# GpSimd in place of ScalarE and VectorE for the split of the last two input pieces

## The chip, the cores and the metric

The kernel runs on one core of a Trainium2 chip. The core has TensorE (PE, matrix multiplies), VectorE (DVE), ScalarE (ACT), GpSimd (POOL) and SyncE (SP, which here only issues DMAs). Every engine works through its own queue in order, and waits on semaphores for the others. The metric is the device time of one launch in microseconds; lower is better.

## The reference

One layer of a streaming encoder, for a prompt of 1024 tokens and a sample of 64 tokens behind a cache of 128. Only its first stage matters here:

```python
qa, ka, va, qi, ki, wi, qb, kb, vb, ga, gb = mixer_inputs(rmsnorm(xp, norm_mix[l]), pos_p, w_in[l], *norms)
# the indexer, per block of 128 queries
s   = relu(einsum('bqhd,bsd->bqhs', q_i, ki_all))      # 8 heads
isc = einsum('bqh,bqhs->bqs', w, s)                     # score of each key
_, idx = lax.top_k(where(vis, isc, -inf), topk)         # 256 best keys
# attention A over the chosen keys, chunk-band attention B, gates, output, MLP
```

The normalised input is multiplied by the weights `w_in`; some of the columns are the indexer's queries, its key and its head weights. Everything behind (heads' projections, choice of keys, two attentions, output projection, MLP) is left as it is.

## The kernel before

**The input.** x is handed over turned (channels on partitions), and loaded in five pieces: four of 256 tokens, and one of 64, the sample. A piece has two tiles `xc` of four blocks of 128 channels each, so 8 blocks k. The division by the row's root mean square is not applied to x; it is applied to the results later. But `norm_mix` (`g_mix`, one number per channel, so per partition) is multiplied in here. Each block is split in a high part (what TensorE's fp32r format holds) and a low part (the remainder), so that three matrix multiplies (`three`, lines 156 to 158: high x high, high x low, low x high) come near fp32. For piece i and block k, `split_piece` does one ScalarE instruction (line 267: scale, round, write the high part into `xnT`) and one VectorE instruction (line 268: raw times `g_mix` minus the high part, the low part).

**The order.** The framework's scheduler places each engine's instructions at build time, by a timeline of its own and by the order of the code; on the chip the queues then run in that fixed order. `cut_piece(i, raws)` runs `split_piece` over the 8 blocks; for pieces 3 and 4 its instructions stand behind `last["queries"]`, the ScalarE copy that ends the queries' projection before. Around the change the code reads:

```python
stage_queries(4, "s"); stage_queries(5, "s")     # 320 columns, PE 33.3 to 39.3 us
... x4 = take_piece(4); stage_scores(0..2)       # scores of blocks 0 to 2
cut_piece(3, x3)                                 # tokens 768 to 1023
norms(4); norms(5); stage_scores(3)
stage_keys(6); stage_keys(7)                     # need piece 3
norms(6); stage_scores(4); stage_queries(6)
cut_piece(4, x4)                                 # the sample's 64 tokens
xsT copy (line 466), stage_keys(8), norms(7), norms(8), stage_queries(7), stage_queries(8)
```

**What the helpers do.** `stage_keys(i)` projects 128 tokens to the indexer's key, three of its query heads and the head weights; the key lands in a tile `kd`. `stage_norms(i)` (called by `norms`) squares the rows of x (line 281, ScalarE, a tile `xt` of 512 KB in two buffers, so a load of `xt` waits for an older square), works out the scale on VectorE, and finishes the key: rotation on GpSimd (`apply_rope`, lines 211 to 214), copy of the key into the second half of `kd` (line 333). `stage_scores(i)` turns the key on TensorE (line 232, into a PSUM tile `pt`), takes high and low parts (`kih` on ScalarE, `kil` on VectorE, line 234), turns the queries `qd` four heads at a time (line 366, into `pt` as well; `qiT` on ScalarE, its low half on VectorE, line 371), and multiplies (lines 164 and 165, into tiles `s`, one per head). ScalarE applies relu (line 379) and VectorE sums over the heads (lines 381 and 383). There are two `pt` banks, taken in turn; a bank is free when VectorE has read it.

**Names.** In the rows of order below, the keys `kd_290`, `kd_295`, `kd_341`, `kd_378` belong to token blocks 0 to 3, `kd_583` and `kd_620` to 4 and 5. `xc_538`, `xc_539` are piece 3; `xc_774`, `xc_775` are piece 4. `xt_668`, `xt_706` are the rows of blocks 4 and 5; block 6 has `xt_904` before and `xt_912` after, block 7 `xt_942` and `xt_950`, the sample `xt_1114` and `xt_1122`. `pt_784`, `pt_788`, `pt_792` hold the turned keys of blocks 0 to 2, `pt_797` and `pt_804` the turned queries of block 2 (heads 0 to 3, 4 to 7), whose scores begin with `s_811`.

Of the kernel before, what the change touches and what calls it, by code (L numbers as in the profile page):

```python
# [15 lines left out]
ALU = mybir.AluOpType  # L16
# [4 lines left out]
KB = D // P  # L21
# [23 lines left out]
def kernel(  # L45
# [8 lines left out]
    nc = tc.nc  # L54
# [68 lines left out]
    def copy(out, in_):  # L123
        return nc.scalar.activation(out, in_, AF.Copy)  # L124

    last = {}
# [91 lines left out]
    g_mix = ixw.tile([P, KB], F32, name="g_mix")  # L218
# [45 lines left out]
    def split_piece(i, raws, k):  # L264
        c0, n = PIECES[i]
        hi, lo, raw = xnT[:, k, 0, c0:c0 + n], xnT[:, k, 1, c0:c0 + n], raws[k // 4][:, k % 4]
        last["piece"] = nc.scalar.activation(hi, raw, AF.Copy, scale=g_mix[:, k:k + 1])
        nc.vector.scalar_tensor_tensor(lo, raw, g_mix[:, k:k + 1], hi, op0=ALU.mult, op1=ALU.subtract)

# [122 lines left out]
    for j in range(KB // 2):  # L392
        parts["keys"] += split_weights(w_keys, j, j % 2 == 1)
        for k in (2 * j, 2 * j + 1):
            split_piece(0, x0, k)
            for i, ps in enumerate(both):
                tok = slice(i * P, (i + 1) * P)
                three(ps[:, :584 - SPLIT], [((xnT[:, k, 0, tok], xnT[:, k, 1, tok]), parts["keys"][k])], k == 0, k == KB - 1)
# [11 lines left out]
        return raws  # L410

    def cut_piece(i, raws):
        with tc.issue_after(last["queries"].ins) if i > 2 else ExitStack():
            for k in range(KB):
                split_piece(i, raws, k)
# [4 lines left out]
    stage_keys(0)  # L420
    stage_keys(1)
    cut_piece(1, x1)
    for i in (2, 3):
        state[i] = project(i, bank("s"), parts["keys"], 584 - SPLIT)[0]
# [12 lines left out]
    norms(1)  # L437
    x3 = take_piece(3)
    cut_piece(2, x2)
    stage_keys(4)  # L440
    stage_keys(5)
# [4 lines left out]
    with tc.issue_after(last["projected"].ins):  # L446
# [6 lines left out]
        for i in range(3):  # L453
            stage_scores(i)
    cut_piece(3, x3)
    norms(4)
    norms(5)
# [279 lines left out]
    for g in range(0, EARLY, 4):  # L737
        ws = []
        for k in range(KB):
            raw = pj.tile([P, 512], F32, tag="wraw", name="wraw", bufs=2)  # L740
            nc.sync.dma_start(raw, w_in[k * P:(k + 1) * P, C_G + g * P:C_G + g * P + 512])
            hi = pj.tile([P, 512], F32R, tag="whi", name="whi", bufs=11)
            lo = pj.tile([P, 512], F32R, tag="wlo", name="wlo", bufs=11)
# [189 lines left out]
    for mix in "ba":  # L933
        for k in range(4):
            for c0, n in CHUNKS:
                raw = op.tile([P, 384], F32, tag="oraw", name="oraw", bufs=2)[:, :n]
                nc.sync.dma_start(raw, o_dram[mix][k * P:(k + 1) * P, c0:c0 + n])
                hi = oT[mix][:, k, 0, c0:c0 + n]
# [96 lines left out]
    for at_m, m in enumerate(pairs_of_m):  # L1035
# [3 lines left out]
        for ci, (c0, n) in enumerate(CHUNKS):  # L1039
# [17 lines left out]
            k, top, low = m % 4, *(("A11", "A21") if m < 4 else ("A12", "A22"))  # L1057
# [4 lines left out]
            if ci == 1:  # L1062
                hi, lo = (row_blocks[top][:, k, z] for z in range(2))
# [602 lines left out]
```

## Time and profile before

| what | value |
| --- | --- |
| runs | 1682.66 us median of 3 (1681.45 to 1686.31) |
| profiled execution | 1685.72 us, of which 1683.9 us are the span of the core |
| TensorE's mean granted clock | 0.997 of full speed |
| PE busy | 1663.4 us (99%) |
| DVE, ACT, POOL busy | 1200.1, 935.4, 388.2 us |
| ScalarE's share of the splits (line 267) | 32 of 128x256 at 500 ns, 8 of 128x64 at 343 ns |
| VectorE's share of the splits (line 268) | 32 of 128x256 at 555 ns, 8 of 128x64 at 318 ns |

A busy share is an average over stages. The stage with the splits lies in the first 60 us: pieces 0 to 2 are split by 28 us, piece 3 from 39.7 to 44.4 us, piece 4 from 56.3 to 59.8 us. The rows that follow are from that stretch. A timeline row gives the start, the length, the engine, the line, what is written and read, and in brackets how long the engine sat idle before it and what it waited for. Lengths overlap a little with the next instruction's start, so a distance from start to start is the better measure of pace.

### The profile page before, as it was taken

The numbers are of one execution on the slowest core, as the hardware profiler recorded it, in microseconds if no ns is written. First come the engines' busy times: TensorE is split into PE (matmuls) and PEld (weight loads), VectorE is DVE, ScalarE is ACT, GpSimd is POOL, SyncE is SP. The second block draws the span as 40 slices with busy tenths as digits, with TensorE's granted clock in tenths as the row PEclk, the third lists the DMA queues.
The fourth block names the chain that finished last, engine by engine and source line by source line (L and its number), as shares of the span: only waits on it lengthen the run. The fifth ranks groups of instructions, "written<-read, shape, count | busy, mean of one in ns | idle before, by whom it ended". The sixth has DMA issues, their size and how long they took to land.

```text
span 1683.9 us, 29511 instructions
## 1 busy us (share of the span) xinstructions
PE 1663.4 (99%) x10037; PEld 1514.3 (90%) x10037; DVE 1200.1 (71%) x2779; ACT 935.4 (56%) x1870; POOL 388.2 (23%) x534
## 2 busy tenths in 40 slices
PE   9899999999999999999999999999999999999999
PEld 8787888788999999999999879999999988888887
DVE  6854898868868888883456785856687649656794
ACT  6866588796157777774244366544454346343431
POOL 4344223504534434431355420000000000000000
PEclk9999999999999999999999999999999999999999
DMA  7234365673398877645655268555575598765652
GB/s 248 62 123 137 98 189 158 178 248 107 108 214 199 207 179 176 165 111 159 193 163 176 88 213 260 177 179 179 186 229 185 194 315 292 224 203 172 204 181 94
DMA packets 276486, 301.99 MB, mean 179 GB/s; under 512 B 40112, under 2 KB 194224, under 8 KB 276336
## 3 DMA queue, kind: packets, MB, share of 16 engines
q1 hardware_dynamic: 247072, 264.39, 54.1%
q10 hardware_dynamic: 29264, 35.73, 6.0%
q8 instruction: 79, 1.29, 0.3%
q14 instruction: 71, 0.58, 0.1%
HBM read 206.93 MB, written 93.08 MB: 178 GB/s over the span
## 4 chain that ended last, share of the span: by engine, by line
PE 70%; DMA 5%; DVE 3%; ACT 2%; issue 1%; POOL 1%; SPq 0%; ACTq 0%; DVEq 0%; POOLq 0%
PE x L156 6%; PE x L157 6%; PE x L158 6%; PE acc L156 5%; PE acc L158 4%; PE acc L157 4%; PE pt L819 3%; PE pe L156 2%; PE pg L156 2%; PE pg L158 2%; PE pe L158 2%; PE pg L157 2%; PE pe L157 2%; PE po L835 2%; PE s L164 2%; PE s L165 2%
## 5 line engine op out<-in xcount | busy, mean ns | idle before, releaser
L124 ACT ACTIVATE hi<-hw 128x1024 fp32r<-128x1024 f32 (+1 forms) x108 | 100.3, 933 | 161.9 <-PE x L158 52.7
L157 PE MATMUL x<-lo,hi 128*128 128x512 f32 (+1 forms) x440 | 169.5, 385 | 0.0
L158 PE MATMUL x<-hi,lo 128*128 128x512 f32 (+1 forms) x440 | 169.1, 385 | 0.0
L156 PE MATMUL x<-hi 128*128 128x512 f32 (+1 forms) x440 | 164.6, 385 | 0.0
L148 DVE TENSOR_TENSOR lo<-hw,hi 128x1024 fp32r<-128x1024 f32 (+1 forms) x108 | 113.9, 1060 | 50.9 <-ACT hi L124 49.8
L622 ACT ACTIVATE nth<-work,cand 128x768 bf16<-128x768 f32 (+2 forms) x93 | 96.6, 1038 | 14.4 <-DVE cand L640 8.1
L831 DVE TENSOR_TENSOR pl<-pt,ph 128x512 fp32r<-128x512 f32 (+2 forms) x152 | 91.1, 614 | 10.8 <-ACT ph L124 10.4
L156 PEld LDWEIGHTS x<-hi 128*128 128x128 f32 x440 | 82.6, 188 | 16.6
L157 PEld LDWEIGHTS x<-lo,hi 128*128 128x128 f32 x440 | 82.7, 188 | 16.6
L158 PEld LDWEIGHTS x<-hi,lo 128*128 128x128 f32 x440 | 82.6, 188 | 16.5
L124 ACT ACTIVATE ph<-pt 128x512 fp32r<-128x512 f32 (+3 forms) x168 | 80.1, 513 | 31.1 <-PE pt L819 22.6
L156 PE MATMUL acc<-xnT,hi 128*128 128x384 f32 (+1 forms) x288 | 96.2, 334 | 0.2 <-DVE gate L689 0.2
L158 PE MATMUL acc<-xnT,lo 128*128 128x384 f32 (+1 forms) x288 | 94.4, 328 | 0.0
L157 PE MATMUL wide<-wlo,xnT 128*128 128x512 f32 x240 | 94.2, 394 | 0.0
L157 PE MATMUL acc<-xnT,hi 128*128 128x384 f32 (+1 forms) x288 | 94.2, 327 | 0.0
L158 PE MATMUL wide<-whi,xnT 128*128 128x512 f32 x240 | 93.8, 391 | 0.0
L156 PE MATMUL wide<-whi,xnT 128*128 128x512 f32 x240 | 92.2, 394 | 0.8 <-DVE work_s L383 0.8
L806 POOL TENSOR_SCALAR mw<-mw,sm 128x640 f32<-128x640 f32 (+1 forms) x64 | 56.4, 882 | 118.2 <-DVE sm L805 106.0
L835 PE MATMUL po<-pl,vhl 128*128 128x256 f32 (+1 forms) x304 | 78.6, 291 | 0.3 <-DVE pl L831 0.3
L834 PE MATMUL po<-ph,vhl 128*128 128x256 f32 (+1 forms) x304 | 77.9, 274 | 0.0
L150 POOL TENSOR_TENSOR wlo<-wraw,whi 128x512 fp32r<-128x512 f32 x40 | 51.7, 1291 | 111.1 <-ACT whi L124 111.0
L164 PE MATMUL s<-kh,qT 128*128 128x384 f32 (+4 forms) x208 | 76.3, 368 | 0.5 <-DVE sm L799 0.5
(775 smaller groups left out, 5630.8 us busy)
## 6 DMA issues: line engine op xcount, KB each, us to landing
hw<-h SPq DMA_DIRECT2D x108, 256.0 KB, 3.2
hw<-in_w_down_dram SPq DMA_DIRECT2D x108, 256.0 KB, 3.6
wraw<-in_w_in_dram SPq DMA_DIRECT2D x56, 256.0 KB, 2.8
h<-h ACTq DMA_DIRECT2D x32, 272.0 KB, 2.1
raw<-in_w_up_dram SPq DMA_DIRECT2D x32, 256.0 KB, 3.3
out_dram<-t SPq DMA_DIRECT2D x24, 256.0 KB, 2.6
raw<-in_w_in_dram SPq DMA_DIRECT2D x24, 256.0 KB, 3.8
g_dram<-gate SPq DMA_DIRECT2D x31, 192.0 KB, 2.7
```

The costliest lines, as they stand in the source:

```text
L124: return nc.scalar.activation(out, in_, AF.Copy)
L148: last["lo"] = nc.vector.tensor_sub(lo, raw, hi)
L150: nc.gpsimd.tensor_sub(lo, raw, hi)
L156: nc.tensor.matmul(out, sh, mh, start=(opens and i == 0), stop=False, skip_group_check=resumes)
L157: nc.tensor.matmul(out, sh, ml, start=False, stop=False, skip_group_check=resumes)
L158: last = nc.tensor.matmul(out, sl, mh, start=False, stop=(closes and i == n - 1), skip_group_check=resumes)
L164: first = nc.tensor.matmul(out, s, mh, start=(i == 0), stop=False)
L622: nc.scalar.activation(sign[:, :w.shape[1]], w, AF.Sign, bias=against, scale=-1.0, accum_out=col(cnt, j))
L806: nc.gpsimd.tensor_scalar(m[:rows, :n], m[:rows, :n], sm[:rows, 6:7], 1.0, op0=ALU.mult, op1=ALU.mult)
L831: nc.vector.tensor_sub(pl[:kr, a:b], ps[:kr, a:b], ph[:kr, a:b])
L834: nc.tensor.matmul(dst, vhl[:krows, vt, :], ph[:krows, oo:oo + width], start=(idx == 0), stop=False)
L835: nc.tensor.matmul(dst, vhl[:krows, vt, :], pl[:krows, oo:oo + width], start=False, stop=(idx == n - 1))
```

## The change

For pieces 3 and 4, GpSimd first multiplies each raw block by `g_mix` in place (8 instructions per piece, not tied to `last["queries"]`); ScalarE then only rounds the product to the high part, and GpSimd subtracts it from the product for the low part. Line 268 is not issued for these pieces: 16 VectorE instructions go, 32 GpSimd instructions come (16 products, 16 differences), and 16 ScalarE instructions stay with another form. No DMA is added or removed.

```diff
     def split_piece(i, raws, k):
         c0, n = PIECES[i]
         hi, lo, raw = xnT[:, k, 0, c0:c0 + n], xnT[:, k, 1, c0:c0 + n], raws[k // 4][:, k % 4]
+        if i > 2:
+            last["piece"] = copy(hi, raw)
+            nc.gpsimd.tensor_sub(lo, raw, hi)
+            return
         last["piece"] = nc.scalar.activation(hi, raw, AF.Copy, scale=g_mix[:, k:k + 1])
         nc.vector.scalar_tensor_tensor(lo, raw, g_mix[:, k:k + 1], hi, op0=ALU.mult, op1=ALU.subtract)
...
     def cut_piece(i, raws):
+        for k in range(KB):
+            raw = raws[k // 4][:, k % 4]
+            if i > 2:
+                nc.gpsimd.tensor_scalar(raw, raw, g_mix[:, k:k + 1], None, op0=ALU.mult)
         with tc.issue_after(last["queries"].ins) if i > 2 else ExitStack():
             for k in range(KB):
                 split_piece(i, raws, k)
```

The scheduler then places much of the stretch from 29 to some 200 us anew. (The lines of after stand 4 or 8 further down: 281 is 285, 333 is 337, 379 is 383.) Three places follow.

GpSimd before, in the stretch from 31 to 35 us, where the keys of blocks 1 and 2 are finished:

```order
L213 TENSOR_TENSOR rb_660<-kd_341,rope_121 128x8
L321 TENSOR_SCALAR sg_591<-sg_591 128x8
L214 TENSOR_TENSOR kd_295<-ra_528,rb_529 128x16
L214 TENSOR_TENSOR kd_341<-ra_659,rb_660 128x16
L333 COPY kd_295<-kd_295 128x64
L211 TENSOR_TENSOR ra_697<-kd_378,rope_121 128x16
L212 TENSOR_TENSOR rb_698<-kd_378,rope_121 128x8
L321 TENSOR_SCALAR sg_628<-sg_628 128x8
L333 COPY kd_341<-kd_341 128x64
```

GpSimd after, the same keys (lines 269 are the differences, lines 420 the products; the eight products of piece 3 and five of piece 4 stand further ahead, in front of the copy of `qd_383`):

```order
L269 TENSOR_TENSOR xnT_105<-xc_538,xnT_105 128x256
L337 COPY kd_290<-kd_290 128x64
L211 TENSOR_TENSOR ra_659<-kd_341,rope_121 128x16
L212 TENSOR_TENSOR rb_660<-kd_341,rope_121 128x8
L213 TENSOR_TENSOR rb_660<-kd_341,rope_121 128x8
L269 TENSOR_TENSOR xnT_105<-xc_538,xnT_105 128x256 x3
L269 TENSOR_TENSOR xnT_105<-xc_539,xnT_105 128x256 x4
L420 TENSOR_SCALAR xc_775<-xc_775,g_mix_133 128x64
L214 TENSOR_TENSOR kd_295<-ra_528,rb_529 128x16
L420 TENSOR_SCALAR xc_775<-xc_775,g_mix_133 128x64 x2
L214 TENSOR_TENSOR kd_341<-ra_659,rb_660 128x16
L337 COPY kd_295<-kd_295 128x64
```

The keys of blocks 0 to 2, finished before the split of piece 3 until now, end behind its differences; the copy of `kd_341` comes four instructions further on.

ScalarE before, from the copy of the last queries on:

```order
L267 ACTIVATE xnT_105<-xc_538,g_mix_133 128x256
L124 ACTIVATE kih_134<-pt_784 128x128
L267 ACTIVATE xnT_105<-xc_538,g_mix_133 128x256
L124 ACTIVATE kih_134<-pt_788 128x128
L267 ACTIVATE xnT_105<-xc_538,g_mix_133 128x256 x2
L267 ACTIVATE xnT_105<-xc_539,g_mix_133 128x256 x4
L281 ACTIVATE xt_668,ss_868<-xt_668 128x1024
L281 ACTIVATE xt_706,ss_906<-xt_706 128x1024
L124 ACTIVATE kih_134<-pt_792 128x128
L124 ACTIVATE qiT_796<-pt_797 128x512
```

ScalarE after, from the same point:

```order
L124 ACTIVATE xnT_105<-xc_538 128x256 x4
L124 ACTIVATE xnT_105<-xc_539 128x256 x4
L285 ACTIVATE xt_668,ss_876<-xt_668 128x1024
L285 ACTIVATE xt_706,ss_914<-xt_706 128x1024
L132 ACTIVATE sd_879<-ss_876,eps_98 128x1
L132 ACTIVATE sd_892<-ss_584,by_row_113 128x1
L132 ACTIVATE sd_917<-ss_914,eps_98 128x1
L132 ACTIVATE sd_930<-ss_621,by_row_113 128x1
L285 ACTIVATE xt_912,ss_1086<-xt_912 128x1024
L132 ACTIVATE sd_1089<-ss_1086,eps_98 128x1
L124 ACTIVATE kih_134<-pt_784 128x128
L314 ACTIVATE jk_1039,ss_1038<-acc_1012 128x64
```

The reads of the turned keys (`kih` from `pt_784` on) moved from between the splits to behind the square of block 6's rows, `xt_912`. On TensorE the turning of the keys of blocks 0 to 2, and of block 2's queries, moved likewise into and behind the keys' projection of blocks 6 and 7; `s_811` has as many rows ahead of it as before.

ScalarE before, around the split of piece 4 (from the copy of block 6's queries into `qd`, whose number is 1034 before and 1042 after):

```order
L124 ACTIVATE qd_1034<-acc_1216 128x5x64
L267 ACTIVATE xnT_105<-xc_774,g_mix_133 128x64 x4
L267 ACTIVATE xnT_105<-xc_775,g_mix_133 128x64 x3
L124 ACTIVATE qiT_948<-pt_956 128x512
L124 ACTIVATE qd_1071<-acc_1041 128x3x64
L319 ACTIVATE aw_1073<-acc_1041 128x8
L267 ACTIVATE xnT_105<-xc_775,g_mix_133 128x64
L281 ACTIVATE xt_942,ss_1299<-xt_942 128x1024
```

ScalarE after, at the same place:

```order
L124 ACTIVATE qd_1042<-acc_1224 128x5x64
L124 ACTIVATE xnT_105<-xc_774 128x64 x4
L124 ACTIVATE xnT_105<-xc_775 128x64
L383 ACTIVATE s_841<-s_841,aw_348 128x384
L124 ACTIVATE xnT_105<-xc_775 128x64 x3
L285 ACTIVATE xt_950,ss_1315<-xt_950 128x1024
L285 ACTIVATE xt_1122,ss_1351<-xt_1122 64x1024
L124 ACTIVATE qiT_956<-pt_964 128x512
```

Here `qiT` of block 3's heads 4 to 7 (`pt_956` before, `pt_964` after) stood behind seven blocks of the split, and stands now behind all eight, one relu and two squares.

## The prediction

> **What bounds the kernel now.** I read the page's first part, then a table by stretches, then TensorE's waits in the stretch of the change, then the timelines of PE, ACT and SP there.
>
> ```profile
> PE 1663.4 (99%) x10037; PEld 1514.3 (90%) x10037; DVE 1200.1 (71%) x2779; ACT 935.4 (56%) x1870; POOL 388.2 (23%) x534
> 36.00:80.00 44.00, 38.48 (x249) 35.28 (x247) 36.13 (x132) 34.57 (x96) 17.54 (x59) 0.96 0.17 50
> 80.00:120.00 40.00, 39.98 (x190) 33.34 (x191) 21.96 (x40) 27.69 (x55) 18.65 (x17) 1.00 0.40 125
> ```
>
> TensorE is the bound: 99% busy, and without a gap from 80 us on for a long time (39.98 of 40; columns: stretch, length, busy PE, PEld, DVE, ACT, POOL, granted clock, DMA share, GB/s). What TensorE loses before 80 us therefore stays lost to the end. It idles 44.00 - 38.48 = 5.5 us between 36 and 80 us, where pieces 3 and 4 are split:
>
> ```profile
> PE pt L366 <- DVE qiT L371: 3.4, 2, 1.8
> PE acc L156 <- ACT xnT L267: 0.7, 1, 0.7
> ...
> 40.23 0.39 PE L156 MATMUL acc<-wkh,xnT 128*128 128x264 f32 x1 [0.70 <-ACT xnT L267]
> 47.12 0.42 PE L164 MATMUL s<-kih,qiT 128*128 128x384 f32 x1
> 48.60 0.27 PE L232 MATMUL pt<-ident,kd 128*128 128x128 f32 x1
> 50.71 0.66 PE L366 MATMUL pt<-ident,qd 128*128 128x128 f32 x4 [1.84 <-DVE qiT L371]
> 51.12 0.39 PE L156 MATMUL acc<-wqh,xnT 128*128 128x320 f32 x1
> 59.34 0.66 PE L366 MATMUL pt<-ident,qd 128*128 128x128 f32 x4 [1.55 <-DVE qiT L371]
> 60.58 0.39 PE L164 MATMUL acc<-wkh,xsT 128*128 128x264 f32 x1 [0.58 <-DVE ms L131]
> ```
>
> Two of these waits (1.84 and 1.55 us) are for a `pt` bank that VectorE has to read (line 371). The second hole (57.8 to 60.6, with four turnings in it) also costs clock (last column but two):
>
> ```profile
> 57.00:58.00 1.00, 0.79 (x4) 0.31 (x2) 1.00 (x6) 1.00 (x6) 0.92 (x4) 1.00 0.16 35
> 61.00:62.00 1.00, 1.00 (x7) 1.00 (x6) 1.00 (x4) 1.00 (x3) 0.00 (x0) 0.51 0.00 0
> 63.00:64.00 1.00, 1.00 (x7) 1.00 (x6) 0.77 (x2) 1.00 (x4) 0.00 (x0) 0.50 0.00 0
> 64.00:65.00 1.00, 1.00 (x7) 1.00 (x7) 0.94 (x4) 0.80 (x4) 0.00 (x0) 0.79 0.00 0
> ```
>
> From 61 to 64.4 us it is half: 0.49 + 0.50 + 0.50 + 0.21 = 1.7 us lost. The hole of 1.84 us cost none.
>
> **The change part by part.** *Prices.* GpSimd's rows:
>
> ```profile
> L150 POOL TENSOR_TENSOR wlo<-wraw,whi 128x512 fp32r<-128x512 f32 x40 | 51.7, 1291 | 111.1 <-ACT whi L124 111.0
> L806 POOL TENSOR_SCALAR m<-m,sm 128x256 f32<-128x256 f32 x16 | 7.7, 480 | 15.1 <-DVE sm L805 7.4 <-PE pt L819 5.9 <-PE po L835 1.8
> L1061 POOL TENSOR_TENSOR A<-gta,gtb 128x256 f32<-128x256 f32 x16 | 12.7, 792 | 0.0
> L333 POOL COPY kd<-kd 128x64 f32<-128x64 f32 x8 | 1.8, 235 | 0.1
> L211 POOL TENSOR_TENSOR ra<-kd,rope 128x16 f32<-128x16 f32 x8 | 1.8, 221 | 14.1 <-DVE by_row L284 6.3 <-PE acc L158 4.5 <-DVE kd L329 2.9
> 41.57 2.82 DVE L268 SCALAR_TENSOR_TENSOR xnT<-xc,g_mix,xnT 128x256 fp32r<-128x256 f32 x6
> ```
>
> A product costs 0.48 us. A difference of 256 columns has no row of its own: half of 1.29 is 0.65, the plain row of that width gives 0.79; I take 0.65 (same types, little VectorE work beside it) and keep 0.79. VectorE paid 0.47 (2.82/6). ScalarE's rounding I take at the old pace, so nothing; the bounds are 0.05 us either way per block, 0.4 in all, and it stands ahead of later work on ScalarE.
>
> *The products.* Piece 3: 8 x 0.48 = 3.8 us near 30 us, once GpSimd has come to them. Behind them stand, in one queue, products of piece 4 and `gain_qb`, which wait for loads:
>
> ```profile
> 29.48 0.86 SPq L246 DMA_DIRECT2D xc<-in_x_turned_dram  x2
> xc<-in_x_turned_dram SPq DMA_DIRECT2D x2, 128.0 KB, 5.5
> 37.05 0.19 POOL L452 TENSOR_SCALAR gain_qb<-gain_qb 128x1 f32<-128x1 f32 x1 [1.69 <-DMA gain_qb<-in_qnorm_b_dram]
> ```
>
> Piece 4 lands at 29.48 + 5.5 = 35 us, `gain_qb` at 37; then one copy and three small ones, so GpSimd is free again at about 38.4, before ScalarE reaches the split at 39.7. The products cost nothing; the cover is that 1.3 us.
>
> *The differences of piece 3.* ScalarE gives the first high part at 40.2. GpSimd: first difference to 40.9, copy of `kd_290` and three small ones (0.24 + 3 x 0.18) to 41.7, seven differences to 46.3, three products of piece 4 (0.28 each) and the rest of `kd_295` to 47.7, `kd_341` to 48.5. TensorE needs 0.73 us per block for two token blocks (6 x 0.122), more than 0.65, so it follows at its own pace and ends the keys of blocks 6 and 7 at about 47.2 (46.9 before, with the turning in between). Cost 0.3, but now no key is turned yet.
>
> *The new wait.* ScalarE reads the turned keys behind the square of `xt_912`, whose load starts when `xt_668` has been squared:
>
> ```profile
> 39.35 0.44 ACT L124 ACTIVATE qd<-s 128x320 f32<-128x320 f32 x1 [3.08 <-PE s L158]
> 40.79 2.50 ACT L267 ACTIVATE xnT<-xc,g_mix 128x256 fp32r<-128x256 f32 x6
> 43.19 1.05 ACT L281 ACTIVATE xt<-xt 128x1024 f32<-128x1024 f32 x1
> 44.36 1.38 SPq L246 DMA_DIRECT2D xt<-in_x_prompt_dram  x2
> 47.99 1.06 ACT L281 ACTIVATE xt<-xt 128x1024 f32<-128x1024 f32 x1 [0.96 <-DMA xt<-in_x_prompt_dram]
> 49.05 0.20 ACT L310 ACTIVATE jk<-acc 128x64 f32<-128x64 f32 x1
> ```
>
> Splits run at (2.50 - 0.50)/5 = 0.40 us, so eight from 39.68 end at 42.88, 0.3 sooner than 43.19. The load is then in 4.80 us later (43.19 to 47.99), at 47.68. Square and sum 1.06, one root 0.19: the first `kih` at 48.93. From there it is a chain through two banks:
>
> ```profile
> L124 ACT ACTIVATE kih<-pt 128x128 fp32r<-128x128 f32 x8 | 2.3, 284 | 0.0
> L234 DVE TENSOR_TENSOR kil<-pt,kih 128x128 fp32r<-128x128 f32 x8 | 2.3, 283 | 0.1
> 57.97 0.58 ACT L124 ACTIVATE qiT<-pt 128x512 fp32r<-128x512 f32 x1
> 58.58 0.69 DVE L371 TENSOR_TENSOR qiT<-pt,qiT 64x512 fp32r<-64x512 f32 x1
> ```
>
> `kih` 0.27 to 49.2, VectorE's chain of block 6 and `kil` (0.28) to 49.9, `pt_792` turned to 50.15; `pt_797` needs the bank of `pt_788` (`kil` to 50.35), four turnings 0.6 to 51.0, `qiT` 0.59 to 51.65, its low half 0.69 to 52.4. `s_811` starts at 52.45 instead of 47.12, 5.3 late. Given back: the 1.84 us wait behind it goes, since both banks are free by 53.1 and the turning comes at 54.1. The queries of block 6 start at 52.45 + 1.48 + 0.15 + 0.41 = 54.5 against 51.12: **+3.4**.
>
> *Around piece 4.*
>
> ```profile
> 55.50 0.56 ACT L379 ACTIVATE s<-s,aw 128x384 f32<-128x384 f32 x1 [0.25 <-PE s L165]
> 55.98 0.43 ACT L124 ACTIVATE qd<-acc 128x320 f32<-128x320 f32 x1
> 56.30 1.77 ACT L267 ACTIVATE xnT<-xc,g_mix 128x64 fp32r<-128x64 f32 x7
> ```
>
> In the old order ScalarE came 0.3 late to `qd` because of the relu at 55.50; that goes (-0.3), so `qd` is copied at 59.04. From there to `qiT`: 0.32 + 5 x 0.24 + 0.47 (relu) + 3 x 0.24 + 2 x 1.04 (squares) = 4.8 us against 1.99 before; `qiT` and its low half, 1.3, free the bank at 6.1, and `xsT` (0.69) is ready at 7.0 behind it. GpSimd's eight differences of 64 columns (0.16 to 0.33 each) end by 3.9 and are covered by the squares; without that cover they would cost up to 1 us. TensorE takes up `xsT` 7.07 us after `qd` instead of 4.60: **+2.5**, less one head's scores more that are done by then (two multiplies of 512 columns; the four heads from 47.12 to 48.60 took 0.37 each at 384, which gives about 0.46). So at this point 3.4 - 0.3 + 2.5 - 0.5 = **+5.1**, at 66.1 us against 60.58.
>
> *VectorE's relief* (8 x 0.47 + 8 x 0.26 = 5.8 us) is worth nothing beyond that: the two waits for line 371 are now set by ScalarE's order. Late next is ScalarE.
>
> *Clock.* The new holes, 47.2 to 52.4 and about 62.2 to 66.1, are both longer than the one from 57.8 to 60.6, which cost 1.7. So one dip more: between 0 (all of it falls in the hole) and 1.7; I take the middle, **+0.9**. Below nothing: the old dip could vanish (-1.7); with a longer hole that is not likely.
>
> *Given back later.*
>
> ```profile
> PE pt L485 <- POOL t L214: 1.8, 3, 1.4
> PE wide L156 <- DVE work_s L383: 0.8, 1, 0.8
> ```
>
> These are nearly all of TensorE's waits from 80 to 470 us. If the others lag less than TensorE, up to 2.6 come back; I take **-0.5**. Sum 5.1 + 0.9 - 0.5 = +5.5. The profiled execution (1685.72) would be 1691.2; the median is 3.1 below it, within its own spread, so I add to the median: 1682.66 + 5.5 = **1688.2**.
>
> The skill speaks against the change at one point where the rows are milder. The row: 0.65 against 0.47 us for a difference, 1.4 times. The Trainium skill, "GPSIMD Engine Reference", section "Engine selection", sends elementwise work to VectorE, since GpSimd is about 2 times slower with two inputs. At 2 x 0.47 = 0.94 (an estimate by the Trainium skill) `kd_341` would be ready at 50.5, which moves the chain by 0.6: 1688.8 by the Trainium skill, 1688.2 by the row. Whether a difference of 256 columns is 1.4 or 2 times as slow no row here shows.
>
> **The rivals.** *Faster.* VectorE's relief pays, and the waits of line 371 go: 1.84 + 1.55 and the dip of 1.7, 5.1 us: 1677.6. It speaks for it that both waits name VectorE. The point of decision is the first `kih` on ScalarE: to hold the old start of the queries at 51.12 it has to come at 48.93 - 3.4 = 45.5, so `xt_912` would have to land 1.5 us or less after its issue instead of 3.6. Chance 0.05.
>
> *Given back.* The same holes, but the dip stays single and falls partly into a hole, and the later waits absorb 2.6: 5.1 - 0.5 - 2.6 = +2: 1684.7. For it: VectorE has 5.8 us less to do. Against it: PE has no gap from 80 to 160 us. Chance 0.22.
>
> *GpSimd sets the pace.* At 0.79 or more a difference (line 1061's row), or 1 us, the keys end at 48 to 49 and `kd_341` at 51; +1.1, two full dips (+1.7) and one lengthened by half an interval (+1): 5.1 + 1.1 + 2.7 = +8.9: 1691.6. Chance 0.15.
>
> **How the numbers follow.** Forecast 0.58, rivals 0.05, 0.22, 0.15. A measurement of this kernel tells about 0.3% from nothing, 5.05 us, so the line is 1687.7; the forecast's own range is 1686 to 1690.5 (dip 0 to 1.7, given back 0 to 2.6), about two thirds above the line. Slower 0.39 + 0.15 = 0.54, same 0.19 + 0.22 = 0.41, faster 0.05. The range reaches to the two nearer rivals, 1684 to 1692, and leaves the faster one and the tails out.
>
> **What would show it.** Right: TensorE waits before the turning of block 1's key and before `s_811`, which starts near 52.4; the square of the third `xt` near 47.7 on ScalarE with nothing behind it until then; `xsT` taken up near 66; the clock at half after each of the two holes; GpSimd's differences near 0.65. Wrong: `kih` from `pt_784` before 46 us, no second dip, or waits of TensorE behind 80 us that shrink by more than 2 us.

## The result: 0.5% slower

The changed kernel takes 1690.78 us (median of 5 runs, 1688.24 to 1694.47), the kernel before 1682.09 us (median of 5, 1681.45 to 1686.31). The ratio is 1.0053 with a 95% interval of 1.0041 to 1.0064, which is 8.9 us (6.9 to 10.8). The forecast was 1688.2 us, in a range of 1684 to 1692.

The two profiled executions shown differ by 2.5 us alone (1688.24 against 1685.72): that of after is the fastest of its runs, that of before one of the slowest. Before was therefore profiled a second time (1680.6 us; the eighth experiment), and traces are compared with that one. First the line of busy times of after, then its stretch from 36 to 80 us (38.48 us busy and a clock of 0.96 before):

```profile
PE 1665.4 (99%) x10037; PEld 1514.1 (90%) x10037; DVE 1197.8 (71%) x2763; ACT 935.1 (55%) x1870; POOL 405.2 (24%) x566
36.00:80.00 44.00, 35.93 (x212) 31.96 (x212) 29.47 (x107) 28.11 (x82) 28.37 (x93) 0.88 0.13 38
```

A mark is needed at which both kernels have done the same work. In every trace of this study 2329 recorded matmuls lie ahead of the first `acc<-xnT,hi` of line 156. That one starts at 461.5 us in before (second profile) and at 469.2 in after, 7.7 us later. The last lines of two tables by stretches, each from 0 to this mark, split the 7.7:

```profile
sum 461.50, PE 452.88 PEld 385.62 DVE 359.71 ACT 309.65 POOL 173.00; mean PE 150.96 PEld 128.54 DVE 119.90 ACT 103.22 POOL 57.67
sum 469.20, PE 456.73 PEld 386.87 DVE 355.54 ACT 308.61 POOL 189.98; mean PE 152.24 PEld 128.96 DVE 118.51 ACT 102.87 POOL 63.33
```

TensorE is busy 456.73 - 452.88 = 3.85 us longer for the same matmuls, so they ran slower, and idles (469.20 - 456.73) - (461.50 - 452.88) = 3.85 us more. In this pair of profiles half of the loss is waiting, and the other half is nearly all lower clock: up to the mark the clock is half for 3.5 us in before (61.5 to 65.0) and for 10.3 us in after, which is 3.4 us of clock more. VectorE's 4.2 us of relief are there too (359.71 to 355.54) and help nobody.

TensorE's waits from 36 to 110 us in after, and its timeline at the two holes:

```profile
PE pt L370 <- DVE qiT L375: 2.4, 1, 2.4
PE pt L232 <- DVE kd L315: 1.4, 1, 1.4
PE pt L232 <- POOL kd L337: 1.2, 1, 1.2
PE pt L370 <- DVE nt L136: 1.0, 1, 1.0
...
48.56 0.33 PE L232 MATMUL pt<-ident,kd 128*128 128x128 f32 x1 [1.15 <-POOL kd L337]
50.27 0.45 PE L232 MATMUL pt<-ident,kd 128*128 128x128 f32 x1 [1.38 <-DVE kd L315]
50.63 1.11 PE L370 MATMUL pt<-ident,qd 128*128 128x128 f32 x4
52.77 1.11 PE L370 MATMUL pt<-ident,qd 128*128 128x128 f32 x4 [1.03 <-DVE nt L136]
54.28 0.69 PE L164 MATMUL s<-kih,qiT 128*128 128x384 f32 x1 [0.40 <-DVE qiT L375]
57.23 0.39 PE L156 MATMUL acc<-wqh,xnT 128*128 128x320 f32 x1
67.18 1.12 PE L370 MATMUL pt<-ident,qd 128*128 128x128 f32 x4 [2.36 <-DVE qiT L375]
68.11 0.59 PE L164 MATMUL acc<-wkh,xsT 128*128 128x264 f32 x1
```

The first hole has three engines in it: the second turned key waits for GpSimd (line 337), the third and the second set of queries for a bank that VectorE has to read. Block 6's queries start at 57.23 instead of 51.12, the sample's keys at 68.11 instead of 60.58. The clock (last column but two) is half from 49.6 to 56.5 us and again from 66.7 to 70.1; three of the windows:

```profile
50.00:51.00 1.00, 0.73 (x3) 0.56 (x4) 0.57 (x4) 0.24 (x1) 1.00 (x5) 0.50 0.72 176
55.00:56.00 1.00, 1.00 (x4) 1.00 (x4) 0.79 (x4) 0.59 (x2) 0.46 (x3) 0.50 0.00 0
68.00:69.00 1.00, 1.00 (x6) 0.90 (x5) 1.00 (x3) 1.00 (x3) 0.25 (x2) 0.50 0.00 0
```

And the rows of GpSimd, ScalarE and VectorE of after that fed the holes:

```profile
28.95 3.66 POOL L420 TENSOR_SCALAR xc<-xc,g_mix 128x256 f32<-128x256 f32 x4
33.02 3.62 POOL L420 TENSOR_SCALAR xc<-xc,g_mix 128x256 f32<-128x256 f32 x4
36.97 2.09 POOL L420 TENSOR_SCALAR xc<-xc,g_mix 128x64 f32<-128x64 f32 x5
40.38 0.72 POOL L269 TENSOR_TENSOR xnT<-xc,xnT 128x256 fp32r<-128x256 f32 x1
41.74 4.89 POOL L269 TENSOR_TENSOR xnT<-xc,xnT 128x256 fp32r<-128x256 f32 x7
48.26 0.25 POOL L337 COPY kd<-kd 128x64 f32<-128x64 f32 x1
49.03 0.23 POOL L337 COPY kd<-kd 128x64 f32<-128x64 f32 x1
...
39.44 2.55 ACT L124 ACTIVATE xnT<-xc 128x256 fp32r<-128x256 f32 x8
46.70 1.06 ACT L285 ACTIVATE xt<-xt 128x1024 f32<-128x1024 f32 x1 [1.88 <-DMA xt<-in_x_prompt_dram]
48.08 0.26 ACT L124 ACTIVATE kih<-pt 128x128 fp32r<-128x128 f32 x1
...
44.68 1.97 DVE L135 SCALAR_TENSOR_TENSOR nt<-r,ms 128x1 f32<-128x1 f32 x1
49.84 0.28 DVE L234 TENSOR_TENSOR kil<-pt,kih 128x128 fp32r<-128x128 f32 x1
51.74 0.23 DVE L315 COPY kd<-acc 128x64 f32<-128x64 f32 x1 [1.17 <-PE pt L370]
```

Thirteen products, 9.4 us of work, fill GpSimd from 29 to 39 us, where before it finished the keys of blocks 0 to 2; these now end at 41.3, 48.5 and 49.3 (31.3, 33.1 and 35.2 before). The first `kih` comes at 48.08, behind the square at 46.70. Its `kil` comes at 49.84 only. And VectorE spends 1.97 us on one instruction of one column, which ends with GpSimd's run of differences at 46.6.

The last row shows a fourth wait. VectorE's copy of block 7's key (line 315) takes one of six `kd` buffers, and can start only when an earlier key has been written out of it. That write-out stands behind the late key: it was issued at 48.45 and landed at 51.62 us. The row names PE; in e1, e3 and e9 the row of this copy names the write-out (`out_dram<-kd`), and there too it starts 0.1 us after the landing. Behind it stand the `kil` that frees the bank for the second set of queries and the low half that `s_811` needs (53.53, though ScalarE had its part ready at 52.4). In before the same write-out was issued at 35.3 and had landed by 37.1 us, and this copy waited for none.

### The profile page after: what moved, and what is told of

It is laid out like the page before. It is cut to its first block, busy times and chain, and to the rows that moved or that the text cites. A ratio compares the mean times of both kernels' runs of the same rounds, so it can differ in the third digit from the quotient of the medians.

```text
span 1686.4 us, 29526 instructions
## 1 busy us (share of the span) xinstructions
PE 1665.4 (99%) x10037; PEld 1514.1 (90%) x10037; DVE 1197.8 (71%) x2763; ACT 935.1 (55%) x1870; POOL 405.2 (24%) x566
## 4 chain that ended last, share of the span: by engine, by line
PE 83%; DVE 1%; ACT 1%; POOL 0%; DMA 0%; issue 0%; ACTq 0%; SPq 0%; DVEq 0%; POOLq 0%
PE acc L156 7%; PE acc L158 7%; PE acc L157 7%; PE x L156 6%; PE x L157 6%; PE x L158 6%; PE pt L827 3%; PE wide L157 3%; PE wide L158 3%; PE wide L156 3%; PE pg L156 2%; PE pg L158 2%; PE po L843 2%; PE pe L158 2%; PE pe L156 2%; PE pg L157 2%
## 5 line engine op out<-in xcount | busy, mean ns | idle before, releaser
L814 POOL TENSOR_SCALAR mw<-mw,sm 128x640 f32<-128x640 f32 (+1 forms) x64 | 56.5, 883 | 118.7 <-DVE sm L813 106.7
```

The lines of the kernel that those rows point to most:

```text
L814: nc.gpsimd.tensor_scalar(m[:rows, :n], m[:rows, :n], sm[:rows, 6:7], 1.0, op0=ALU.mult, op1=ALU.mult)
```

## The experiments

Twelve more runs were made, e1 to e12 (e8, the kernel before once more, gives only a profile). Ratios are to runs of before on the same chip; us are the ratio less 1, times 1681. The mark is that of the one profiled execution (462.0 and 461.5 in the two of before, 469.2 in after). It is of one execution and differs from the ratio by up to 2.8 us (e2, e3, e7, where the verdict is the ratio's).

| run | what | median us | ratio (95%) | us | mark |
| --- | --- | --- | --- | --- | --- |
| e1 | change at piece 3 alone | 1686.13 | 1.0028 (1.0017 to 1.0040) | +4.7 | 466.7 |
| e2 | change at piece 4 alone | 1681.80 | 1.0003 (0.9994 to 1.0012) | +0.5 | 464.8 |
| e3 | GpSimd products, VectorE differences | 1684.88 | 1.0025 (1.0016 to 1.0034) | +4.2 | 468.3 |
| e4 | VectorE products, GpSimd differences | 1682.77 | 1.0010 (1.0001 to 1.0019) | +1.7 | 464.0 |
| e5 | GpSimd: keys first | 1688.51 | 1.0044 (1.0031 to 1.0056) | +7.4 | 469.2 |
| e6 | ScalarE: square last | 1687.03 | 1.0039 (1.0026 to 1.0051) | +6.6 | 467.5 |
| e7 | before, squares last | 1678.89 | 0.9989 (0.9980 to 0.9998) | -1.8 | 462.3 |
| e9 | VectorE: norm with one input | 1689.55 | 1.0059 (1.0046 to 1.0071) | +9.9 | 471.4 |
| e10 | e5, e6, e9 and more together | 1682.19 | 1.0016 (1.0007 to 1.0026) | +2.7 | 462.2 |
| e11 | before, squares last, norm with one input | 1680.54 | 1.0000 (0.9991 to 1.0009) | 0 | 461.0 |
| e12 | e10 without e9 | 1683.35 | 1.0014 (1.0005 to 1.0023) | +2.4 | 463.6 |

**e1 and e2: where.** The condition `i > 2` becomes `i == 3`, or `i > 3`, at both places.

> Only piece 3 is treated by GpSimd; piece 4 is split as before (ScalarE scales, VectorE takes the low parts). Theory (order): the time goes where the finishing of keys 1 and 2 is pushed behind GpSimd's new work at 29 to 47 us, which opens the first hole and starts a clock dip; here that queue is nearly the same, so most of the 8.7 us stay: 6 to 9 us slower than before, block 6's queries near 57 us (57.2 in the changed kernel, 51.1 before). Rival (GpSimd's pace: its instructions as such are too slow, so that the loss follows the work moved): piece 3 has 1.61 of 2.0 us of GpSimd work per pair of blocks, so about 7 us as well, and the other 1.7 with piece 4. Rival (clock alone): one dip instead of two, about half, 4 us.

> Only piece 4 (64 tokens) is treated by GpSimd; piece 3 is split as before. Theory (order): the eight products stand in GpSimd's queue between the finishing of the keys, but cost 8 x 0.42 = 3.4 us near 35 to 38 us and push the copies of keys 1 and 2 by that; the first turned key is still read between the splits, the second behind a square. A smaller first hole, and at piece 4 the qiT behind two squares: 1 to 4 us slower. Rival (GpSimd's pace): 8 differences of 0.3 us under ScalarE's squares, no loss that can be measured, within 1 us of before. Rival (VectorE's relief): 1 to 2 us faster, since VectorE has 16 instructions of 0.3 us less at the wait of line 371.

Both cost less than the theory said: piece 3 alone 4.7 us (2.9 to 6.7, expected 6 to 9), piece 4 alone nothing that can be told from zero, as its first rival had it; together they cost 8.9. So piece 3 carries the larger part, and the two aren't independent: with both, five of piece 4's products (2.09 us at 36.97 above) stand between the keys as well, which may be the reason. Of e1's three expectations "clock alone" (4 us) came nearest, and the trace agrees: up to the mark TensorE idles 12.1 us, nearly as long as in after (12.5; 8.6 in before), but is busy 2.1 us less than in after, and the clock is half in one stretch (52.1 to 58.9 us) instead of two. In e1 the first hole is there with another face, now named by VectorE's reading of a bank:

```profile
51.38 0.66 PE L370 MATMUL pt<-ident,qd 128*128 128x128 f32 x4 [3.19 <-DVE kil L234]
```

**e3 and e4: which half of GpSimd's work.**

```diff
-            nc.gpsimd.tensor_sub(lo, raw, hi)           # e3
+            nc.vector.tensor_sub(lo, raw, hi)
-                nc.gpsimd.tensor_scalar(raw, raw, g_mix[:, k:k + 1], None, op0=ALU.mult)   # e4
+                nc.vector.tensor_scalar(raw, raw, g_mix[:, k:k + 1], None, op0=ALU.mult)
```

> GpSimd does only the products of pieces 3 and 4; ScalarE rounds them, and VectorE takes the low parts by a plain difference. Theory (order, by the products): the 7.3 us of products of piece 3 and 2.1 us of piece 4 stand in front of the finishing of keys 0 to 2 in GpSimd's queue (28.9 to 39 us), so that these keys still end behind 40 us, the first turned key is read behind the square of block 6's rows, and the hole before block 2's scores stays: 6 to 10 us slower, block 6's queries begin at 55 to 58 us. Rival (the differences of 0.70 us on GpSimd, against 0.31 us a rounding, set the pace): they are gone here, so within 2 us of before.

> GpSimd does only the differences; the products of pieces 3 and 4 are taken by VectorE ahead of the split. Theory (order, by the products): GpSimd has nothing new before 40 us, the keys 0 to 2 are finished at 31 to 35 us as before, and their reading stands between ScalarE's roundings again, so the first hole does not open: from 2 us faster to 2 us slower than before, block 6's queries at 50 to 52.5 us. Rival (GpSimd's differences set the pace): keys of blocks 6 and 7 end behind eight differences of 0.70 us with four instructions on the queries between, and most of the loss stays, 4 to 9 us slower.

With the products alone 4.2 us are lost (below the 6 to 10 expected), with the differences alone 1.7. The products matter more, by their place: in e3 the keys of blocks 1 and 2 end late (45.5 and 46.0 us) although no difference stands in front of them, and TensorE waits 2.97 us at 52 us. In e4 the keys end at 31 to 35 us as before, and the first hole is gone; what is lost there is lost at the second place, where the sample's keys start at 66.22 (60.7 before) behind a norm of VectorE. Block 6's queries start at 54.72, later than expected, since the scores of four more heads now stand ahead of them. The group rows of e4 and of after give the prices of the same product on both engines:

```profile
52.09 1.97 PE L370 MATMUL pt<-ident,qd 128*128 128x128 f32 x8 [2.97 <-DVE kil L234]
...
66.22 0.59 PE L164 MATMUL acc<-wkh,xsT 128*128 128x264 f32 x1 [1.77 <-DVE by_row L287]
...
L420 DVE TENSOR_SCALAR xc<-xc,g_mix 128x256 f32<-128x256 f32 x8 | 2.7, 374 | 0.0
L420 POOL TENSOR_SCALAR xc<-xc,g_mix 128x256 f32<-128x256 f32 x8 | 7.3, 922 | 0.0
```

**e5: undo GpSimd's order alone.** Differences and piece 4's products are placed behind the copy of block 2's key.

```diff
+        last["key", i] = nc.gpsimd.tensor_copy(kd[:rows, 1, :], kd[:rows, 0, :])
+                with tc.issue_after(last["key", 2].ins) if i > 3 else ExitStack():   # products of piece 4
+            with tc.issue_after(last["key", 2].ins):                                 # differences
```

> The changed kernel, with the same instructions, but GpSimd's copy of the key of block 2 stands ahead of the differences of piece 3 and of the products of piece 4; only the eight products of piece 3 are still ahead of the keys. Theory (GpSimd's queue): keys 0 to 2 are finished at about 40.5 us instead of 41 to 49, the differences run from 41.5 to 47.5 (0.7 each), the keys of blocks 6 and 7 end near 48, about 1 us later than in the changed kernel, but the turned keys and queries of block 2 are ready by then; TensorE has no hole before block 2's scores and the first dip goes: 5 to 6 of the 8.7 us come back, 2 to 4 us slower than the kernel before. Rival (GpSimd's instructions as such are too slow): all of them are still there and the differences end later, so it stays 8 to 10 us slower.

This expectation failed. The keys end at 38.8, 39.8 and 40.3 us, as meant, but 7.4 us stay. The scheduler, knowing of the early keys, put the third turning in TensorE's queue ahead of most of the keys' matmuls of blocks 6 and 7. It needs a bank that ScalarE has not read (two squares stand in front) and VectorE neither (its norm is held for 1.85 us). A 6 us wait takes the place of the old holes:

```profile
47.26 0.45 PE L232 MATMUL pt<-ident,kd 128*128 128x128 f32 x1 [6.00 <-DVE nt L135]
...
45.05 1.85 DVE L135 SCALAR_TENSOR_TENSOR nt<-r,ms 128x1 f32<-128x1 f32 x1
```

**e6: undo ScalarE's order alone.** In `row_stats`, for block 6 (`last["qiT", 2, 1]` is ScalarE's reading of block 2's second set of turned queries):

```diff
-        with tc.issue_after(last["piece"].ins):
+        with tc.issue_after(last["qiT", 2, 1].ins if i == 6 else last["piece"].ins):
```

> The changed kernel, with one thing moved on ScalarE: the square of block 6's rows stands behind the reading of block 2's turned queries (qiT). Theory (GpSimd's queue): keys 1 and 2 are copied at 48.3 to 50.8 us whatever ScalarE does, so the chain of turned keys ends as late; at most 1 us comes back, 7 to 9 us slower than before. Rival (the wait for the square, as the prediction priced it: the first kih behind the square): the first kih comes near 45 instead of 48.1 us and the chain with it, 3 us come back, 5 to 6 us slower.

The first `kih` moves from 48.08 to 45.13, as the rival said, and yet the next turning waits for GpSimd's copy as before:

```profile
45.13 0.26 ACT L124 ACTIVATE kih<-pt 128x128 fp32r<-128x128 f32 x1
...
48.98 0.33 PE L232 MATMUL pt<-ident,kd 128*128 128x128 f32 x1 [1.11 <-POOL kd L337]
```

Block 2's scores start at 52.37 instead of 54.28, and the mark comes 1.7 us earlier: in this one profile the square has a share of about a fifth. The ratio (6.6 us, 4.4 to 8.6) covers both expectations.

**e9: change VectorE's narrow norm alone.** Line 135 read two tiles of one column from SBUF; it and line 137 now read one, and take the other as a scalar.

```diff
-            nc.vector.scalar_tensor_tensor(nt, r0, r0, ms, op0=ALU.mult, op1=ALU.mult)
+            nc.vector.tensor_scalar(nt, r0, r0, ms, op0=ALU.mult, op1=ALU.mult)
-            nc.vector.tensor_mul(rs, nt, r0)
+            nc.vector.tensor_scalar(rs, nt, r0, 1.0, op0=ALU.mult, op1=ALU.mult)
```

> The changed kernel; in the narrow norm (lines 135 and 137, one column) VectorE's two instructions that read two tiles from SBUF are written as a multiply by scalars, with one tile read. The orders of TensorE, ScalarE and GpSimd up to 70 us are the same. Theory (VectorE is held by GpSimd): the row of 1.97 us for one column at 44.68, which ended with GpSimd's run of differences, was a wait for GpSimd; in the new form it takes 0.2, VectorE's chain and the kil of key 0 behind it come 1 to 1.8 us earlier, the third turning near 49.3 instead of 50.3, 1 to 2 us come back: 6 to 8 us slower than before. Rival (the order alone): the row stays long, or its queue waits for kih anyway, and nothing comes back: 8 to 9.5 us slower.

This instruction is no longer held: 0.26 us in the middle of GpSimd's run, against 1.97. The time does not follow (9.9 us, 7.7 to 11.9). The third turning comes at 49.82 instead of 50.27 and then waits for GpSimd's copy; the second set of queries is turned at 52.72, against 52.77. The trace shows two reasons. VectorE is still held until the run of differences ends, at 47.3 us here, now at the next instruction with two tiles (line 333, 1.12 us against 0.29 for the next one), so the hold is shortened and not undone. And the copy of line 315 waits for the write-out of a key again, until 51.87:

```profile
44.74 0.26 DVE L135 TENSOR_SCALAR nt<-r,ms 128x1 f32<-128x1 f32 x1
46.25 1.12 DVE L333 SCALAR_TENSOR_TENSOR kd<-kd,rs,g_ki 128x64 f32<-128x64 f32 x1
51.87 0.23 DVE L315 COPY kd<-acc 128x64 f32<-128x64 f32 x1 [1.75 <-DMA out_dram<-kd]
...
49.82 0.33 PE L232 MATMUL pt<-ident,kd 128*128 128x128 f32 x1 [0.34 <-POOL kd L337]
52.72 1.11 PE L370 MATMUL pt<-ident,qd 128*128 128x128 f32 x4 [1.66 <-DVE nt L136]
```

**e10 and e12: undo the orders together, leave the work.** e10 has the edits of e5, e6 and e9, and the squares of blocks 4 and 5 tied behind the `kih` of block 1 (`last["kih", P]`). All 32 GpSimd instructions are still there. e12 is e10 without the edit of e9.

```diff
-        with tc.issue_after(last["piece"].ins):
+        with tc.issue_after(last["qiT", 2, 1].ins if i == 6 else last["kih", P].ins if i in (4, 5) else last["piece"].ins):
```

> The changed kernel with every instruction on the engine where the change put it, but with the waits taken away together: GpSimd finishes keys 0 to 2 ahead of the differences and of piece 4's products; ScalarE reads the turned keys 0 and 1 ahead of the squares of blocks 4 and 5, and block 2's queries ahead of block 6's square; the narrow norm in the form with one input. Theory (order and VectorE held, on three queues together): keys turned near 41 are read at 42.3, the third turning comes near 43 (47.3 in the kernel with the keys first), the scores of block 2 stand between the keys of blocks 6 and 7, whose queries start near 51 as in before: from 1 us faster to 3 us slower than before. Rival (GpSimd's instructions as such are too slow): all 32 are still there, in the same place, and 5 to 9 us stay.

> The kernel with all waits undone, but the narrow norm in its old form with two tiles read (the order of all engines up to 70 us is the same). If VectorE being held by GpSimd's run of differences costs time on the path, line 135 at 45.6 us is held to 47.0, the low half of the turned queries behind it comes at 47.6 instead of 46.1, and the kernel is 1 to 3 us slower than that one: 3.5 to 5.5 us slower than before. If GpSimd's and ScalarE's orders alone carry the loss, the hold is hidden behind the keys of blocks 6 and 7, which TensorE computes until 48 us: 1 to 3.5 us slower than before, as that one (2.4).

In e10, 2.7 us are left of 8.9 (1.2 to 4.4), and the mark comes at 462.2, 0.7 us behind before. The first rows are e10's third turning and its table's last line to the mark (idle 8.3 us, 8.6 in before; busy 1.0 us more); the last two are e12's:

```profile
43.08 0.30 PE L232 MATMUL pt<-ident,kd 128*128 128x128 f32 x1 [1.74 <-DVE kil L234]
sum 462.20, PE 453.91 PEld 387.06 DVE 355.73 ACT 309.03 POOL 190.89; mean PE 151.30 PEld 129.02 DVE 118.58 ACT 103.01 POOL 63.63
...
45.40 2.41 DVE L135 SCALAR_TENSOR_TENSOR nt<-r,ms 128x1 f32<-128x1 f32 x2
48.65 0.69 PE L164 MATMUL s<-kih,qiT 128*128 128x384 f32 x1 [1.97 <-DVE qiT L376]
```

So the same instructions on the same engines cost 2.4 us in one order (e12; 0.8 to 3.9) and 8.9 in the other. That is the main result: about 6 of 8.9 us are order. What is left is not exactly the price of GpSimd's work as such, since the order of e10 and e12 isn't that of before: block 6's square stands behind the turned queries, and the squares of blocks 4 and 5 have moved too. The nearest kernels without GpSimd's work (below) have the former move and not the latter: e10 is 2.7 us above e11, and e12 some 4 above e7. In e12 VectorE is held again (2.41 us for two instructions), and there TensorE does wait 1.97 us for what stands behind; its mark is 1.4 us later than e10's. The times can't tell the two apart (+2.4 and +2.7, each with 1.5 us either way), so what the hold costs stays open between 0 and about 2 us.

**e7, e8 and e11: the kernel before.** e7 and e11 tie the squares of blocks 6 to 8 in the kernel before behind the reading of the turned queries; e11 has e9's edit as well. e8 is before, unchanged.

> The kernel before, with only ScalarE's order changed: the square of block 6's rows stands behind the reading of block 2's turned queries (qiT), those of block 7 and of the sample behind that of block 3. If ScalarE's order sets the wait of 1.84 us for line 371 (the second qiT at 49.24 us stood behind that square, which ended at 49.0), the wait goes and block 6's queries start near 49.3 instead of 51.1: 1 to 4 us faster than before. If VectorE sets that wait, nothing changes.

> The kernel before, unchanged, for a second profiled execution. If the 2.4 us that the changed kernel wins back between 812 and 907 us, and the 1.9 between 1000 and 1027, are chances of the one profiled execution of before (which was 3.6 us above its median), the second profile has 92.7 us in the first of these stretches as all later ones have, and something else than 28.1 in the other; 1680 to 1683 us. If the late stages really absorb a delay, it has 95.2 us there again.

> The kernel before, without GpSimd in the split, with ScalarE's squares behind the reading of the turned queries (as in the earlier run of that order, which was 1.9 us faster) and the narrow norm in the form with one input. If VectorE being held costs before something on the path too, 2 to 4 us faster than before; if it is only the order, 1 to 2 us faster, as without it.

e7 came out as its first expectation said, at the slow end (1.8 us). e11 came out as neither said: nothing, with 1.5 us either way. In e7 the second `qiT` comes at 47.52 instead of 49.24, and the wait of 1.84 us shrinks to 0.18, so ScalarE's order set it, not VectorE:

```profile
47.52 0.60 ACT L124 ACTIVATE qiT<-pt 128x512 fp32r<-128x512 f32 x1
...
49.17 0.66 PE L366 MATMUL pt<-ident,qd 128*128 128x128 f32 x4 [0.18 <-DVE qiT L371]
```

e7 is the fastest kernel here, by 1.8 us against before (0.3 to 3.4) and by some 11 against after (8.9 and 1.8). With e9's edit added nothing is gained (e11), so the 1.8 are not secured as a gain of this order; that edit also makes the scheduler place much else anew, so e11 doesn't single it out.

e8 answers where the profile pair's difference went. The stretch from 812 to 907 us, of before, e8 and after:

```profile
812.00:907.00 95.00, 93.14 (x562) 92.50 (x561) 49.12 (x94) 33.82 (x78) 47.71 (x55) 1.00 0.52 157
812.00:907.00 95.00, 95.00 (x576) 94.59 (x575) 49.38 (x94) 35.06 (x79) 49.35 (x56) 1.00 0.49 151
812.00:907.00 95.00, 95.00 (x579) 95.00 (x578) 48.94 (x94) 35.17 (x81) 47.78 (x53) 1.00 0.52 161
```

Only the first profile of before idles there (its 1.86 us). From the mark to the start of the last `x<-hi` matmul of line 156 it took 1218.1 us; e8 took 1213.5, after 1213.4, and the others 1210.9 to 1215.1. Nothing is given back behind the mark; the first profile had a bad second half.

## Why the prediction was right, and where it was not

The direction, the mechanism (order, then holes, then clock) and the range held. The size was 5.5 us for a measured 8.9, and the measured 1690.78 lies in the range only because that was widened to the rivals: the forecast's own span ended at 1690.5, and its bounds (dip 0 to 1.7, given back 0 to 2.6) really give 1685.2 to 1689.5. By its steps:

- **Products, 0.48 us each, cover 1.3 us.** Mis-sized: 0.91 from start to start at 256 columns (3.66 for four), 0.42 at 64. The row of line 806, of the same width and engine, has a second operation and yet half the price; why wasn't tried. GpSimd was free at 40.4 instead of 38.4, so the cover was gone, and the eight products are 7.3 us instead of 3.8.
- **Differences, 0.65 us each.** 0.70 (4.89 for seven). Nearly right; VectorE's plain difference takes 0.46 (e3: 3.69 for eight), so 1.5 times. The Trainium skill, "GPSIMD Engine Reference", section "Engine selection", has about 2 times for two inputs and roughly line rate for one. The trace has it the other way round: 1.5 times for the difference, and for the product with one tile 922 against 374 ns, 2.5 times.
- **Keys of blocks 6 and 7 end at 47.2; first `kih` at 48.93.** 47.4 and 48.08. The first is right. The second came 0.85 earlier, since ScalarE's plain rounding runs at 0.31 us (2.55 for eight) where I kept the scaled one's 0.40, and so the square came 1 us earlier, at 46.70.
- **`s_811` at 52.45.** 54.28: the step that failed in the first hole. From `kih` to `kil` I counted VectorE's short chain, 1 us to the end of `kil`; it took 2.0 (48.08 to 50.12), behind a chain that GpSimd had held until 46.6. And I priced the four turnings at 0.6 us, at full clock; the dip had begun in the hole, and they took 1.11. The rest I had not counted at all: the low half of the first queries started 1.15 us after ScalarE's part, since VectorE had stood 1.17 us at line 315 for the write-out of the late key and had block 7's norm to do first.
- **Queries of block 6, +3.4.** 57.23 - 51.12 = +6.1: `s_811` came 1.8 later than forecast, and another 0.9 went because the scores in between ran at half clock too.
- **Around piece 4, +2.5.** From the copy of `qd` to `xsT` 68.11 - 61.79 = 6.32 instead of 7.07 (4.60 before), so +1.7. The roundings are quicker; the hidden differences stayed hidden.
- **Clock, +0.9.** Here the sum failed most. TensorE's busy time rose by 3.85 us, 3.4 of it by the clock's own record, while its waiting rose by 3.85, less than the 5.1 of the sum. I took a dip as one stretch of 3.4 us at half clock; the first lasted from 49.6 to 56.5, twice that, with two further waits inside it (1.03 and 0.40 us).
- **Given back, -0.5.** Nothing, by the mark.
- **VectorE's relief, nothing.** Right. The wait of 1.84 us is worth something only when ScalarE's order changes (e7).

Of the rivals, GpSimd's pace came nearest in its number (1691.6), for a reason that e12 refutes: with the same instructions in a better order 6 us come back. My own theory for the experiments, that GpSimd's queue alone carries the loss, fell with e5. The place has three queues that each hold the bank chain: GpSimd's copies of the keys (with their write-out behind them), ScalarE's squares, VectorE's held norm. Changed alone, none gave back more than 2.3 us (VectorE's was only shortened by e9); GpSimd's and ScalarE's together (e12, with the squares of blocks 4 and 5 too) gave back 6.5.

## What to carry to other kernels

Work moved to an engine with idle time is paid by what stands behind it in that engine's queue: look for the small instructions there that others wait for, before pricing the arithmetic. Where several queues feed one chain, undoing one order alone may show nothing, and the scheduler turns the relief into another wait; test the joint undo before a theory is dropped. Price a hole at TensorE with the half clock that follows it, including the instructions inside the hole.

## What the runs showed of the hardware

GpSimd can hold VectorE until a whole run of instructions ends. A VectorE instruction of one column with two tiles read took 0.21 us with GpSimd idle (before, 47.34), and 1.97 (after), 1.85 (e5) and 2.41 for two of them (e12) within GpSimd's differences; in after and e5 it ended with the run of them, at 46.6 and 46.9 us; with one tile read it took 0.26 within the same run (e9). So back-to-back GpSimd instructions of 0.70 us let nothing in between. GpSimd's products did not hold it so: four such instructions within a run of them, of 0.9 us each, took 0.19 to 0.50 us (after, from 28.98 on). The Trainium skill, "SBUF — State Buffer", section "Who interferes with whom", states that a VectorE instruction with two SBUF inputs contends with a GpSimd instruction that reads SBUF, and calls the shared ports an exclusive lock. The trace agrees for the differences; the products read SBUF too, and there the measurement decides. I had not counted this wait.
